# HGRN2 heads ahead of mLSTM heads in a hybrid decoder layer, and two raw tiles for the down factors

## The chip, the cores and the metric

The kernel runs on one core of a Trainium2 chip. The metric is the device time of one execution in microseconds, the median of several. Five engines work side by side, each through its own instructions in program order: TensorE (PE; its weight loads are PEld), VectorE (DVE), ScalarE (ACT), GpSimd (POOL) and SyncE (SP), which issues most DMAs.

## The reference

One step of a decoder layer: 1024 prompt positions and 8 decode sequences of 4 positions, 1056 columns in all. Width 1024, feed-forward width 2816, all in fp32. The mixer has four mLSTM heads and four HGRN2 heads side by side, 128 wide each:

```python
h = _rmsnorm(x, norm_mix)
p = jnp.einsum('btd,dp->btp', h, w_in) + b_in
qk_a, v_a, o_a, i_a, f_a, q_b, f_b, i_b, g_b = jnp.split(p, offs, axis=-1)
out_a, buf, C, n, m = _mlstm_mixer(qk_a, v_a, o_a, i_a, f_a, conv_buf, C0, n0, m0, conv_w, conv_b, mlstm_norm)
out_b, S = _hgrn_mixer(q_b, f_b, i_b, g_b, S0, lb, hgrn_norm)
mix = jnp.concatenate([out_a, out_b], axis=-1).astype(x.dtype)
x = x + jnp.einsum('btm,md->btd', mix, w_out)
h2 = _rmsnorm(x, norm_ffn)
ff = jax.nn.silu(jnp.einsum('btd,df->btf', h2, w_gate)) * jnp.einsum('btd,df->btf', h2, w_up)
x = x + jnp.einsum('btf,fd->btd', ff, w_down)
```

An mLSTM head passes q and k through a causal convolution of width 4 and a silu, and scans a matrix memory with input and forget gates that all four heads share (`i_raw`, `f_raw`, with a log-sigmoid and a running maximum). An HGRN2 head scans a state whose decay is its own for each feature (`f = lb + (1 - lb) * sigmoid`). Both end in a head norm and an output gate. The outputs are the final norm of x and all states, for the prompt and for the decode sequences.

## The kernel before

**Columns and units.** The 1056 columns stand in three blocks of 288 (256 prompt and the 32 decode columns), 384 and 384. An fp32 product is made of three matmuls of rounded halves (L135 hi by hi, L136 lo by hi, L137 hi by lo). A *unit* is one tile of 128 output features by one block: 8 slices of the contraction by 3, 24 matmuls. When a unit is done its `evac` moves it out of PSUM and its `post` may start a generator.

**Order.** The program is written out once by Python, and that order is the order on every engine. Side work (norms, gates, mixers, preparation of factors) is a set of generators. `hook()` is called every two slices, four times a unit; a generator that said `yield n` goes on n hooks later. `finish(key)` runs hooks until a generator is done. So a row's place on DVE or ACT follows from its number of hooks behind a unit, and what stands ahead of it there is done ahead of it.

**Stages.** Startup norms the three blocks of x: block 0 at once (`startup0`), 1 and 2 by `startup(1)` and `startup(2)` beside the first units. 99 units follow: the gate tile and 16 tiles of the mLSTM heads, then 16 tiles of the HGRN2 heads, each for three blocks. Of a head and block, the units are q, k, v, o (mLSTM) or f, q, v, g (HGRN2). Then come w_out (from the constant `first_wo`), two plain feed-forward pairs and 20 feature tiles in a two-level Winograd scheme (gate and up from about 700 us, then down), and a final norm.

**Around the change.** `gates(ps, b)` (L288) turns the gate unit of a block into log-decays (L308 to L310 on ACT: Abs, Exp, Ln; L312 to L329 on DVE, with scans), exponentials (L331 to L333) and columns by PE transposes (L343 to L346). Its numbers of hooks are `GAW`. `conv` (L432) makes q and k: three DVE rows (L445), a tanh (L449) and L450. `mix_a(h, b)` scans a block of an mLSTM head, 20 hooks long in its last row of `MAW`; its state update is L557 and L559, its products with the state L570 and L572. `mix_b(h, b)` does so for an HGRN2 head in 32 hooks: pairwise steps at levels 1, 2, 4 up to 64, each of two DVE rows (L794 on q, L796 on k, with a small row L802), and PE products for each level (L775, L853, L858), transposes of k (L875), the state's input (L889) and the products with it (L909, L911). `sample_a` and `sample_b` do the decode columns through `sample_core`, with state loads, products (L644, L672) and updates (L649) for each of 8 sequences. In before `sample_a` makes its updates at once and `sample_b` puts them off to the w_out units.

In the Winograd stage `wd_prep` prepares the factors of w_down: 20 groups, each with one load of 512 KB to the tile `fr` (L1389), four roundings on ACT to tiles `fh` (L1396), their rests on DVE (L1401) and stores to DRAM (L1402), and additions on DVE between them. `fr` has one buffer, so the load of a group is issued when the last one's reads are done, `WDY[2]` = 5 hooks ahead of its first rounding. `fh` has three.

Of the kernel before, what the change touches and what calls it, by code (L numbers as in the profile page):

```python
# [40 lines left out]
def hybrid_step(ctx: ExitStack, tc: tile.TileContext, i, o):  # L41
# [244 lines left out]
    GAW = ((1, 6, 14), (2, 3, 6), (2, 3, 6))  # L286

    def gates(ps, b):  # L288
# [15 lines left out]
        while b == 0 and ("cv", "k") not in done:  # L304
            yield 1
# [31 lines left out]
        if b == 0:  # L337
            start(gates_sample(ig, lf), ("gsm",), 40)
# [14 lines left out]
    def gates_sample(ig, lf):  # L353
# [36 lines left out]
        for a in ATs + ADs:  # L390
            nc.gpsimd.memset(a, 0.0)
# [10 lines left out]
    ss_ = {n_: mp.tile([128, 4, 32], F32, name=n_) for n_ in ("sq", "sk", "sv", "so")}  # L402

    def conv_evac(kind, h, b):
        j = h if kind == "q" else 4 + h

        def ev(ps):
            n, npr = BL[b], NPR[b]
            raw = mp.tile([128, 387], F32, tag="raw", name="raw", bufs=2)
            if kind == "q" and b and (h or b == 2):  # L410
                finish(("pS", h, b - 1))
            acc = early(kind, h, b)
            if acc is None:
                acc = tl("c" + kind, 384, 1 if kind == "q" else 2)
# [8 lines left out]
            if (h, b) == (0, 0):  # L423
                start(conv(kind, h, b, raw, acc, rs), ("cv", kind), 1)
            else:
                for _ in conv(kind, h, b, raw, acc, rs):
                    pass
        return ev

    def conv(kind, h, b, raw, acc, rs):  # L430
        j = h if kind == "q" else 4 + h
        n, npr = BL[b], NPR[b]  # L432
        while ("rs", 2) not in done:
            yield 1
# [16 lines left out]
        if b == 0:  # L451
            nc.gpsimd.tensor_copy(ss_["s" + kind][:, h, :], acc[:, 256:288])

    def early(name, h, b):
        if (name, h, b) == ("v", 0, 0):
            return ktm.rearrange("p h t -> p (h t)")
        if name != "q" or h or b == 2:
            return None
        return mp.tile([128, 4, 130], F32, tag="st", name="st", bufs=2).rearrange("p a c -> p (a c)")

    def act_evac(name, tag, func, bj, h, b, bufs=1, silu=False):
        def ev(ps):
            n = BL[b]
            t = early(name, h, b)
            if t is None:
                t = tl(tag, 384, bufs)
# [8 lines left out]
            if b == 0 and name in ("v", "o"):  # L475
                nc.gpsimd.tensor_copy(ss_["s" + name][:, h, :], t[:, 256:288])
# [13 lines left out]
    def norm_cols(s, sqs, nch, d2=None, p=128):  # L490
# [9 lines left out]
    MAW = (  # L500
# [4 lines left out]

    def mix_a(h, b):
        w = MAW[b if h == 0 else 3]
# [3 lines left out]
        while ("gc", b) not in done or ("cv", "k") not in done:  # L511
            yield 1
# [22 lines left out]
        if (h, b) == (0, 0):  # L535
            nc.gpsimd.memset(ktm, 0.0)
# [53 lines left out]
        nc.vector.scalar_tensor_tensor(mo(b)[:, h, :], pH[:, :npr], col(V_MN + h), S["o", h, b][:, :npr],  # L590
# [75 lines left out]

# [33 lines left out]
    def sample_a():  # L700
        qS, kS = ss_["sq"], ss_["sk"]
# [17 lines left out]
        for h in range(H):  # L719
# [12 lines left out]
    atn = [0]  # L732
    gS = mp.tile([128, 4, 8], F32, name="gS")
# [13 lines left out]
    def mix_b(h, b):  # L747
# [8 lines left out]
        qB, kB = tl("qB"), tl("kB")  # L756
# [62 lines left out]
        if samp:  # L819
            while ("sa",) not in done:  # L820
                yield 1
            nc.vector.tensor_copy(ss_["sk"][:, h, :], kB[:, 256:288])
            nc.vector.tensor_copy(gS[:, h, :], gx[:, gst[1] + 64:gst[1] + 72])
            nc.vector.tensor_copy(ss_["sq"][:, h, :], qB[:, 256:288])
# [56 lines left out]
        if samp:  # L881
            nc.gpsimd.tensor_copy(ss_["sv"][:, h, :], v[:, 256:288])
            nc.gpsimd.tensor_copy(ss_["so"][:, h, :], S["g", h, b][:, 256:288])
# [44 lines left out]
        nc.vector.scalar_tensor_tensor(mo(b)[:, 4 + h, :], pH[:, :npr], col(V_HN + h), S["g", h, b][:, :npr],  # L928
                                       op0=OP.mult, op1=OP.mult)

    def sample_b():
        yield from sample_core(4, 128, V_HN, i["S0"], lambda h, s: gS[:, h, s:s + 1], o["Ss"], None, None, None,
                               later=("su",))
# [12 lines left out]
    ti = 0  # L946
    wa = i["wA"]
    tg = wtile(wa[0])
# [1009 lines left out]
```

## Time and profile before

| | |
|---|---|
| median of 3 runs | 1400.34 us (1400.12 to 1401.76) |
| profiled execution, its own time | 1404.88 us |
| span of its profile | 1403.1 us |
| mean granted TensorE clock | 0.978 |
| the first mLSTM head, all three blocks | within the first 130 us |
| first `fr` load to last | 742.1 to 1068.9 us |

Busy is the time in which an engine worked. The granted clock is TensorE's, 1.00 for full speed; at 0.50 a matmul takes twice as long and still counts as busy. A list of waits says which engine and line stood idle, what released it, how long in all, how often, and the longest. The rows that matter are shown in the prediction.

### The profile page before, as it was taken

The page shows a single profiled execution, that of the slowest core. Times are in us where ns is not written, and L with a number is a line of the kernel's source. Part 1 is how long each engine was busy: PE and PEld are TensorE (multiplying, and loading weights), DVE is VectorE, ACT ScalarE, POOL GpSimd, SP SyncE. Part 2 cuts the span into 40 slices and gives each one's busy share as a digit, 9 for nine tenths or more (in the row PEclk, how much of TensorE's full clock was granted, in tenths as well). Part 3 has the DMA queues.
Part 4 walks back from the last instruction along what each step waited for, and adds up shares of the span by engine and source line. Part 5 has one row for each costly group of instructions (what it writes and reads, how often), then busy time and mean ns, then how long its engine had stood idle before and what let it go on. Part 6 is the DMA issues. An engine that isn't in the chain of part 4 may idle for free. (4 is left out here: it accounts for less than half of the span.)

```text
span 1403.1 us, 29356 instructions
## 1 busy us (share of the span) xinstructions
PE 1338.5 (95%) x11600; PEld 1305.5 (93%) x11600; DVE 882.1 (63%) x2060; ACT 554.3 (40%) x1315; POOL 593.6 (42%) x566
## 2 busy tenths in 40 slices
PE   7888999999999999999989999999999999999996
PEld 6778999899999997999989999999999999999995
DVE  7876657664555556634576666666775346777765
ACT  6554334234334335323444544444444341122232
POOL 5223212232222314123447656665655683444434
PEclk8999999999999999999999999999999999999997
DMA  6012122330111114543544656756656278878733
GB/s 224 23 43 70 53 60 73 96 99 21 44 47 34 39 41 131 155 152 124 185 146 174 245 189 215 247 193 215 235 176 224 77 260 319 308 269 299 274 143 124
DMA packets 108882, 212.11 MB, mean 151 GB/s; under 512 B 10801, under 2 KB 63561, under 8 KB 108233
## 3 DMA queue, kind: packets, MB, share of 16 engines
q1 hardware_dynamic: 108312, 209.98, 43.6%
q8 instruction: 91, 1.49, 0.4%
q14 instruction: 47, 0.38, 0.1%
q10 hardware_dynamic: 432, 0.27, 0.1%
HBM read 143.76 MB, written 66.45 MB: 150 GB/s over the span
## 5 line engine op out<-in xcount | busy, mean ns | idle before, releaser
L135 PE MATMUL mm<-HI,whi 128*128 128x384 f32 (+2 forms) x1160 | 379.1, 327 | 6.6 <-ACT gA L302 2.9
L137 PE MATMUL mm<-HI,wlo 128*128 128x384 f32 (+2 forms) x1160 | 363.2, 313 | 1.3 <-POOL wlo L97 1.3
L136 PE MATMUL mm<-LO,whi 128*128 128x384 f32 (+2 forms) x1160 | 363.0, 313 | 0.5 <-POOL LO L225 0.2
L135 PEld LDWEIGHTS mm<-HI,whi 128*128 128x128 f32 x1160 | 221.5, 191 | 11.8 <-ACT gA L302 3.2
L136 PEld LDWEIGHTS mm<-LO,whi 128*128 128x128 f32 x1160 | 221.5, 191 | 1.4 <-POOL LO L225 0.9
L137 PEld LDWEIGHTS mm<-HI,wlo 128*128 128x128 f32 x1160 | 221.2, 191 | 1.8 <-POOL wlo L97 1.8
L97 POOL TENSOR_TENSOR wlo<-raw,whi 128x512 fp32r<-128x512 f32 x90 | 118.7, 1329 | 214.7 <-ACT whi L96 169.8
L1189 POOL TENSOR_TENSOR wlo<-S,whi 128x512 fp32r<-128x512 f32 x78 | 108.4, 1396 | 112.2 <-ACT whi L1188 102.1
L1260 PE MATMUL mx<-T,whi 128*128 128x264 f32 x640 | 118.4, 284 | 1.7 <-DVE sg L1227 0.9
L1401 DVE TENSOR_TENSOR fh<-fr,fh 128x512 fp32r<-128x512 f32 x80 | 76.4, 959 | 68.3 <-ACT fh L1396 67.6
L1260 PEld LDWEIGHTS mx<-T,whi 128*128 128x128 f32 x640 | 99.0, 188 | 2.1 <-DVE sg L1227 1.1
L1313 POOL TENSOR_TENSOR LO<-rg,HI 128x528 fp32r<-128x528 f32 x52 | 70.5, 1367 | 65.4 <-ACT HI L1312 65.4
L1260 PE MATMUL mx<-HI,whi 128*128 128x264 f32 x320 | 92.1, 288 | 4.1 <-ACT u L1268 4.1
L1260 PE MATMUL mx<-HI,wlo 128*128 128x264 f32 x320 | 91.6, 286 | 0.0
L1260 PE MATMUL mx<-LO,whi 128*128 128x264 f32 x320 | 91.4, 286 | 0.0
L1260 PE MATMUL mx<-T,wlo 128*128 128x264 f32 x320 | 90.8, 284 | 0.0
L1487 DVE TENSOR_TENSOR X<-X,mx 128x264 f32<-128x264 f32 x160 | 65.5, 425 | 27.2 <-PE mx L1483 26.7
L1188 ACT ACTIVATE whi<-S 128x512 fp32r<-128x512 f32 x80 | 50.3, 631 | 73.4 <-DVE S L1177 73.4
L1312 ACT ACTIVATE HI<-rg 128x528 fp32r<-128x528 f32 x52 | 32.3, 641 | 104.6 <-PE mx L1483 34.1
L1396 ACT ACTIVATE fh<-fr 128x512 fp32r<-128x512 f32 x80 | 45.3, 571 | 69.6 <-DMA fr<-in_wd 43.0
L1260 PE MATMUL mm<-HI,wlo 128*128 128x264 f32 x240 | 68.2, 284 | 0.0
L1260 PE MATMUL mm<-HI,whi 128*128 128x264 f32 x240 | 68.2, 284 | 0.0
(545 smaller groups left out, 3449.6 us busy)
## 6 DMA issues: line engine op xcount, KB each, us to landing
d_wf<-fh SPq DMA_DIRECT2D x60, 512.0 KB
rg<-d_ff SPq DMA_DIRECT2D x42, 528.0 KB
raw<-in_wA SPq DMA_DIRECT2D x31, 512.0 KB
whi<-d_wf SPq DMA_DIRECT2D x29, 512.0 KB
wlo<-d_wf SPq DMA_DIRECT2D x28, 512.0 KB
raw<-in_wgu SPq DMA_DIRECT2D x24, 512.0 KB
d_ff<-sg SPq DMA_DIRECT2D x40, 264.0 KB
rg<-in_wgu SPq DMA_DIRECT2D x20, 512.0 KB
```

The source lines that it names most:

```text
L97: (nc.gpsimd if pool else nc.vector).tensor_tensor(lo[:, s], raw[:, s], hi[:, s].bitcast(F32), op=OP.subtract)
L135: nc.tensor.matmul(ps[:, :n], wh, rh[:, k, :], start=(k == 0), stop=False)
L136: nc.tensor.matmul(ps[:, :n], wh, rl[:, k, :], start=False, stop=False)
L137: nc.tensor.matmul(ps[:, :n], wl, rh[:, k, :], start=False, stop=(k == nk - 1))
L1188: nc.scalar.activation(hi[:, s], t, AF.Copy)
L1189: (nc.vector if dve else nc.gpsimd).tensor_tensor(lo[:, s], t, hi[:, s].bitcast(F32), op=OP.subtract)
L1260: nc.tensor.matmul(ps[:, :QN], a[:, w], b_[:, kk, c], start=new and kk == 0 and x == 0, stop=kk == 3 and x == 2, skip_group_check=True)
L1312: nc.scalar.activation(h, src, AF.Copy)
L1313: (nc.vector if dve else nc.gpsimd).tensor_tensor(lw, src, h.bitcast(F32), op=OP.subtract)
L1396: nc.scalar.activation(h, src, AF.Copy)
L1401: nc.vector.tensor_tensor(lw, src, h.bitcast(F32), op=OP.subtract)
L1487: nc.vector.tensor_tensor(y, y, ps[:, :QN], op=OP.add)
```

## The change

The units of the HGRN2 heads come first (48 units) and the gate tile and mLSTM heads behind them. The host orders the weight tiles, w_out's rows and so the features of `X` to match. `sample_b` starts four units ahead of the first mLSTM unit, with its state updates at once; `sample_a` waits for it, and puts its updates off. `gates` has tiles of its own and one row of hooks for all blocks, `mix_a` one row for all heads, `conv` runs at once in the evacuation. The norms of blocks 1 and 2 must be done at units 4 and 8 (5 and 10), and their squares use other scratch. Apart from that, `wd_prep` has two `fr` tiles and loads a group right behind the first store of the group before; `fh` has two buffers, and a group one hook less.

```diff
@@ -283,26 +283,18 @@
-    GAW = ((1, 6, 14), (2, 3, 6), (2, 3, 6))
+    GAW = ((2, 3, 6), (2, 3, 6), (2, 3, 6))
...
         lo, hi = slice(0, 4), slice(32, 36)
-        if b == 0:
-            A, B = (a.rearrange("p c t -> p (c t)") for a in ATs)
-            Cc, me = (mp.tile([128, 3, 130], F32, tag="C", name="C", bufs=2).rearrange("p a c -> p (a c)")
-                      for _ in range(2))
-            me = me[0:4]
-        else:
-            A, B, Cc = (mp.tile([36, 384], F32, tag=x, name=x) for x in ("gA", "gB", "gC"))
-            me = mp.tile([4, 385], F32, tag="gm", name="gm")
+        A, B, Cc = (mp.tile([36, 384], F32, tag=x, name=x, bufs=nb) for x, nb in (("gA", 2), ("gB", 2), ("gC", 1)))
+        me = mp.tile([4, 385], F32, tag="gm", name="gm", bufs=1)
         ig, f, lf, a = A[lo, :n], A[hi, :n], B[lo, :n], B[hi, :n]
...
         yield 1
-        while b == 0 and ("cv", "k") not in done:
-            yield 1
         while b and ("pS", 0, b - 1) not in done:
@@ -335,7 +327,7 @@
-            start(gates_sample(ig, lf), ("gsm",), 40)
+            start(gates_sample(ig, lf), ("gsm",), 4)
...
@@ -420,18 +408,12 @@
-            if (h, b) == (0, 0):
-                start(conv(kind, h, b, raw, acc, rs), ("cv", kind), 1)
-            else:
-                for _ in conv(kind, h, b, raw, acc, rs):
-                    pass
+            conv(kind, h, b, raw, acc, rs)
...
-        while ("rs", 2) not in done:
-            yield 1
...
@@ -497,18 +470,14 @@
-    MAW = (
-        (1, 1, 3, 3, 2, 2, 2, 6, 1),
-        (2, 3, 3, 1, 2, 4, 1, 7, 3),
-        (3, 1, 3, 1, 2, 2, 2, 4, 1),
-        (2, 1, 3, 1, 2, 2, 2, 6, 1))
+    MAW = (2, 1, 3, 1, 2, 2, 2, 6, 1)
...
-        w = MAW[b if h == 0 else 3]
+        w = MAW
...
-        while ("gc", b) not in done or ("cv", "k") not in done:
+        while ("gc", b) not in done:
@@ -532,8 +501,8 @@
-        if (h, b) == (0, 0):
-            nc.gpsimd.memset(ktm, 0.0)
+        while (h, b) == (0, 0) and ("b", H - 1, 2) not in done:
+            yield 1
...
@@ -596,10 +565,11 @@
-    def sample_core(h_off, w, vnorm, st_in, decay, out_state, n_io, d2, k_scale, later=None):
-        qS, kS, vS, oS = (ss_[x] for x in ("sq", "sk", "sv", "so"))
+    nc.gpsimd.memset(ktm, 0.0)
+    def sample_core(ss, h_off, w, vnorm, st_in, decay, out_state, n_io, d2, k_scale, later=None, end=None):
+        qS, kS, vS, oS = (ss[x] for x in ("sq", "sk", "sv", "so"))
@@ -658,11 +628,15 @@
                 nc.vector.tensor_scalar_mul(vm[:, 0:w], vt[:, 0:w], seqm[:, s:s + 1])
+                if w == 129:
+                    nc.gpsimd.tensor_copy(sts[s][:, :, 128:129], n_io[0][:, 4 * s:4 * s + 4, None])
                 yield 3
...
                 yield 3
+            if end is not None:
+                end()
@@ -698,7 +672,9 @@
-        qS, kS = ss_["sq"], ss_["sk"]
+        while ("sb",) not in done:
+            yield 1
+        qS, kS = ssA["sq"], ssA["sk"]
@@ -721,15 +697,17 @@
-        yield from sample_core(0, 129, V_MN, i["C0"], lambda h, s: wiS[:, 32 * h + 4 * s + 3:32 * h + 4 * s + 4],
-                               o["Cs"], (nT, no), scol[:, 1:2], scol[:, 2:3])
-        nc.sync.dma_start(o["ns"], no)
+        yield from sample_core(ssA, 4, 129, V_MN, i["C0"], lambda h, s: wiS[:, 32 * h + 4 * s + 3:32 * h + 4 * s + 4],
+                               o["Cs"], (nT, no), scol[:, 1:2], scol[:, 2:3], later=("su",),
+                               end=lambda: nc.sync.dma_start(o["ns"], no))
...
+    for a in ATs + ADs:
+        nc.gpsimd.memset(a, 0.0)
...
@@ -943,32 +918,32 @@
-    ti = 0
...
-    tg = wtile(wa[0])
...
-        ts = [wtile(wa[1 + 4 * h + j]) for j in range(4)]
+        ts = [wtile(wa[4 * h + j]) for j in range(4)]
+        for b in range(NB):
+            evs = [f_evac(h, b), act_evac("qb", "cq", AF.Sigmoid, V_BIN + 16 + h, h, b, 2, silu=True),
+                   act_evac("vb", "v", AF.Identity, V_BIN + 24 + h, h, b, 2),
+                   act_evac("g", "go", AF.Sigmoid, V_BIN + 28 + h, h, b, 2, silu=True)]
+            posts = [None, spawn((lambda h, b: lambda: mix_b(h, b))(h, b), "b", h, b), None, None]
+            in_group(ts, b, evs, posts, (("mm", "mm", "mx", "mx") if (h, b) == (0, 0) else None))
+    first_a = len(units)
+    tg = wtile(wa[16])
+    for h in range(H):
+        ts = [wtile(wa[17 + 4 * h + j]) for j in range(4)]
...
-                   act_evac("v", "v", AF.Identity, V_BIN + 8 + h, h, b),
+                   act_evac("v", "v", AF.Identity, V_BIN + 8 + h, h, b, 2),
...
-            in_group(ts, b, evs, posts, (("mm", "mm", "mx", "mx") if (h, b) == (0, 0) else None))
+            in_group(ts, b, evs, posts)
...
-    for h in range(H):
-        ts = [wtile(wa[17 + 4 * h + j]) for j in range(4)]
-        for b in range(NB):
-            evs = [f_evac(h, b), act_evac("qb", "cq", AF.Sigmoid, V_BIN + 16 + h, h, b, silu=True),
-                   act_evac("vb", "v", AF.Identity, V_BIN + 24 + h, h, b),
-                   act_evac("g", "go", AF.Sigmoid, V_BIN + 28 + h, h, b, 2, silu=True)]
-            posts = [None, spawn((lambda h, b: lambda: mix_b(h, b))(h, b), "b", h, b), None, None]
-            in_group(ts, b, evs, posts)
...
@@ -1384,14 +1359,14 @@
         def fload(g):
-            t = fpool[0].tile([128, 4, 256], F32, tag="fr", name="fr", bufs=1)
+            t = fpool[0].tile([128, 4, 256], F32, tag="fr", name="fr", bufs=2)
             f = NPLAIN + 4 * (g // 4)
...
             n = 128 * src.shape[1]
-            t = fpool[0].tile([128, 1024], F32R, tag="fh", name="fh", bufs=3)
+            t = fpool[0].tile([128, 1024], F32R, tag="fh", name="fh", bufs=2)
             h, lw = (x.rearrange("p (f c) -> p f c", c=128) for x in (t[:, 0:n], t[:, n:2 * n]))
@@ -1400,14 +1375,17 @@
             nc.sync.dma_start(d_wf[g, k, :, 0:2 * n], t[:, 0:2 * n].bitcast(F32))
-        r = fload(0)
+        nxt = fload(0)
         yield WDY[0]
         for g in range(NG):
+            r = nxt
             left, right = r[:, :, 0:128], r[:, :, 128:256]
...
             rest(g, 0, left, p)
+            if g + 1 < NG:
+                nxt = fload(g + 1)
             p = rnd(a22)
@@ -1425,12 +1403,9 @@
-            yield WDY[1]
-            if g + 1 < NG:
-                r = fload(g + 1)
...
-    WDY = (2, 2, 5)
+    WDY = (2, 2, 6)
@@ -1667,12 +1642,12 @@
-        acc = (ntile("W") if b == 1 else tl("vt", 390, 1))[:, :n]
+        acc = ntile()[:, :n]
...
-            sq = tl(*SQT[(0, 1, 6, 7)[m % 4]])[:, :n]
+            sq = (ntile("raw") if m % 4 < 2 else tl("qB"))[:, :n]
...
@@ -1826,13 +1800,11 @@
             finish(("w", u["t"]))
-        if ui in (5, 10):
-            finish(("n1", ui // 5))
-        if ui == b0_first - 8:
-            lb_consts()
-        if ui == b0_first + 4:
-            finish(("sa",))
-        if ui == b0_first + 12 * (H - 1) + 8:
+        if ui in (4, 8):
+            finish(("n1", ui // 4))
+        if ui == first_a - 8:
+            conv_consts()
+        if ui == first_a - 4:
             start(sample_b(), ("sb",))
...
```

DVE in the first 60 us. Before, behind norm 1 (L228, L225), the convolution of the first head's q follows:

```order
L225 TENSOR_TENSOR LO<-X,HI 128x384
L228 SCALAR_TENSOR_TENSOR X<-X,vec,mx 128x384 x2
L225 TENSOR_TENSOR LO<-X,HI 128x384
L209 TENSOR_SCALAR nrs<-mx 128x3
L435 COPY raw<-hist 128x3
```

The same place of the change (`nt` is the sum of squares of block 2, `qw`, `ck`, `qB`, `kB` are q and k of `mix_b`):

```order
L209 TENSOR_SCALAR nrs<-mx 128x3
L1653 TENSOR_TENSOR nt<-raw 128x384
L1653 TENSOR_TENSOR nt<-nt,qB 128x384 x2
L1653 TENSOR_TENSOR nt<-nt,raw 128x384 x2
L1653 TENSOR_TENSOR nt<-nt,qB 128x384 x2
L789 COPY_PREDICATED AD_127<-msk,mx 128x64
...
L772 TENSOR_TENSOR qw<-qw,ngb 128x144
L774 TENSOR_TENSOR ck<-ck,ngb 128x144
L780 TENSOR_TENSOR wib<-ngb 128x144
...
L228 SCALAR_TENSOR_TENSOR X<-X,vec,mx 128x384 x2
```

Seven sum rows stand ahead of the first steps of `mix_b(0, 0)` (L772, L774), and these ahead of norm 1 (L228).

DVE of the change at units 49 and 50, where the first gates (`gA`, `gB`, `gC`, `gm`) meet the end of the last `mix_b` (in before the first gates met a convolution there):

```order
L619 SCALAR_TENSOR_TENSOR st<-st,gS,mx 128x128 x4
L304 SCALAR_TENSOR_TENSOR gB<-gA,gB 4x288
L305 COPY gm<-mcar 4x1
L309 SCALAR_TENSOR_TENSOR gC<-ones,gB 4x128 x2
L311 SCALAR_TENSOR_TENSOR gm<-gB,mcar,gA 4x256
L312 COPY mcar<-gm 4x1
...
L321 TENSOR_TENSOR gA<-gA,gC 4x256
L772 TENSOR_TENSOR qB<-qB,wib 128x3x64
L774 TENSOR_TENSOR kB<-kB,wib 128x3x64
L780 TENSOR_TENSOR wib<-wib 128x3
L417 COPY raw<-hist 128x3
```

The step at level 64 (L772, L774) stands behind the gates and behind an update of `sample_b` (L619), and the convolution of q (from L417) behind it. On PE the transposes of that kB (L851) come at U50.

SP in the Winograd stage, before:

```order
L1389 DMA fr<-in_wd 128x4x256
L1402 DMA d_wf<-fh 128x1024
L1402 DMA d_wf<-fh 128x512
L1241 DMA d_ff<-sg 128x528
L1402 DMA d_wf<-fh 128x1024 x2
L1389 DMA fr<-in_wd 128x4x256
```

and now:

```order
L1364 DMA fr<-in_wd 128x4x256
L1377 DMA d_wf<-fh 128x1024
L1364 DMA fr<-in_wd 128x4x256
L1377 DMA d_wf<-fh 128x512
L1216 DMA d_ff<-sg 128x528
L1377 DMA d_wf<-fh 128x1024 x2
```

The load of the next group moves from behind a group's four stores to behind its first.

More of the change, by code (lines that the diff above doesn't have):

```diff
@@ L409, in ev @@
             raw = mp.tile([128, 387], F32, tag="raw", name="raw", bufs=2)
[L410 to L414, printed above, removed]
+            if kind == "q" and b == 2:
+                finish(("pS", h, 0))
+            acc = tl("c" + kind, 384, 2)
             S[kind, h, b] = acc
@@ L819, in mix_b @@
         if samp:
-            while ("sa",) not in done:
-                yield 1
-            nc.vector.tensor_copy(ss_["sk"][:, h, :], kB[:, 256:288])
+            nc.vector.tensor_copy(ssB["sk"][:, h, :], kB[:, 256:288])
             nc.vector.tensor_copy(gS[:, h, :], gx[:, gst[1] + 64:gst[1] + 72])
-            nc.vector.tensor_copy(ss_["sq"][:, h, :], qB[:, 256:288])
+            nc.vector.tensor_copy(ssB["sq"][:, h, :], qB[:, 256:288])
         yield 2
@@ L988, in mix_split @@
         for m in range(KT):
-            while any(("a" if m < 4 else "b", m % 4, b) not in done for b in range(2 + th)):
+            while any(("b" if m < 4 else "a", m % 4, b) not in done for b in range(2 + th)):
                 yield 2
@@ L998, in mix_split @@
         if th:
-            while ("sb",) not in done:
+            while ("sa",) not in done:
                 yield 1
@@ L1712, in hybrid_step @@
     startup0()
-    conv_consts()
+    lb_consts()
     for _ in split(1, True):
@@ L1912, in _prepare @@
     idx = [4 * g + h for h in range(4) for g in range(4)] + [16 + 4 * g + h for h in range(4) for g in (1, 0, 2, 3)]
-    wA = np.concatenate([tiles(gate), wt[idx]], axis=0)
+    wA = np.concatenate([wt[idx[16:]], tiles(gate), wt[idx[:16]]], axis=0)
     bg = np.zeros((128, 1), b_in.dtype)
```

34 lines of the change are left out of this document (11 added, 23 removed).

## The prediction

> **What bounds the kernel now.** I read the page's first part, then busy time by stretches of 50 us, then TensorE's waits in the stretches that are not full. Columns of the stretches: length, then busy time and number of instructions of PE, PEld, DVE, ACT and POOL, granted clock, DMA share, GB/s.
>
> ```profile
> PE 1338.5 (95%) x11600; PEld 1305.5 (93%) x11600; DVE 882.1 (63%) x2060; ACT 554.3 (40%) x1315; POOL 593.6 (42%) x566
> 50.00:100.00 50.00, 38.15 (x217) 36.08 (x216) 37.91 (x83) 30.97 (x58) 12.38 (x16) 0.90 0.06 14
> 100.00:150.00 50.00, 44.94 (x298) 43.91 (x297) 33.10 (x103) 20.49 (x58) 13.41 (x21) 0.97 0.27 82
> 150.00:200.00 50.00, 50.00 (x338) 49.94 (x337) 32.84 (x88) 19.70 (x55) 13.66 (x18) 1.00 0.20 60
> 250.00:300.00 50.00, 47.33 (x354) 43.65 (x353) 33.31 (x100) 15.80 (x38) 17.37 (x41) 1.00 0.41 125
> 300.00:350.00 50.00, 48.45 (x567) 45.91 (x566) 25.01 (x99) 18.31 (x60) 9.70 (x12) 1.00 0.08 24
> 400.00:450.00 50.00, 49.74 (x631) 47.41 (x632) 27.69 (x104) 21.98 (x69) 14.21 (x13) 1.00 0.11 35
> 550.00:600.00 50.00, 48.05 (x489) 45.76 (x490) 30.76 (x97) 18.15 (x53) 9.40 (x13) 0.97 0.51 152
> ```
>
> TensorE bounds it: 95% busy, and full at 150 to 200. The change has no other matmuls, so it can only move the places where PE idles or runs at a lower clock. The largest is the first mLSTM head: 50 to 100 lacks 11.9 us and 100 to 150 lacks 5.1. The clock costs 38.15 x 0.10 = 3.8 and 44.94 x 0.03 = 1.3. That is **22.1 us** in all, 5.1 of clock on 17.0 of idleness: 0.30 us of clock for each idle us. The HGRN2 heads (400 to 450) lack 0.3 in 50. DVE works 33 us in 50 in an mLSTM stretch and 26 to 28 in an HGRN2 one. The waits in the poor place (waited in all, times, longest):
>
> ```profile
> PE mx L572 <- DVE C L557: 3.7, 1, 3.7
> PE mm L135 <- ACT gA L302: 2.9, 1, 2.9
> PE mx L549 <- issue: 1.8, 1, 1.8
> PE mx L344 <- ACT gB L332: 3.4, 1, 3.4
> ```
>
> L135 and L344 wait for the gates; L572 for an mLSTM state behind DVE's convolution. They belong to the first mLSTM head while DVE is also making norms.
>
> **The change, part by part.** I write U50 for the point at which 50 units are done. Each sum is made against the profiled execution (1404.88 us) and then added to the median (1400.34).
>
> *A, the start.* HGRN2 units now run while blocks 1 and 2 are normed. What goes is the loss behind 72.5 us, where before has done nine units:
>
> ```profile
> 75.00:80.00 5.00, 1.17 (x9) 0.97 (x8) 3.56 (x9) 2.97 (x4) 0.00 (x0) 0.98 0.00 0
> 80.00:85.00 5.00, 3.31 (x19) 3.06 (x20) 2.78 (x11) 2.37 (x8) 0.75 (x2) 0.50 0.30 77
> 85.00:90.00 5.00, 5.00 (x28) 5.00 (x27) 3.73 (x11) 1.82 (x4) 0.00 (x0) 0.84 0.03 9
> 90.00:95.00 5.00, 4.26 (x28) 4.02 (x27) 3.30 (x8) 4.87 (x9) 0.00 (x0) 1.00 0.00 0
> 105.00:110.00 5.00, 1.28 (x12) 0.93 (x11) 2.56 (x15) 3.97 (x8) 0.00 (x0) 1.00 0.05 16
> 110.00:115.00 5.00, 4.84 (x25) 4.68 (x24) 2.61 (x10) 2.59 (x13) 4.42 (x8) 0.66 0.51 157
> 115.00:120.00 5.00, 4.34 (x33) 4.11 (x33) 3.89 (x8) 2.92 (x7) 2.48 (x3) 1.00 0.08 15
> 120.00:125.00 5.00, 4.47 (x34) 4.31 (x35) 4.25 (x16) 1.47 (x4) 0.21 (x1) 1.00 0.50 157
> ```
>
> Idle: 3.8 + 1.7 + 0.7 + 3.7 + 0.2 + 0.7 + 0.5 = 11.3. Clock: 3.31 x 0.50 + 5.00 x 0.16 + 4.84 x 0.34 = 4.1. Together 15.4. An HGRN2 head with norms done should lose about 1.5 in the same work (0.3 in 50, and a little for DVE). What comes: the seven DVE rows that sum the squares of block 2 now stand ahead of the first steps of mix_b, and those steps ahead of norm 1.
>
> ```profile
> 33.04 3.03 DVE L1678 TENSOR_TENSOR vt<-vt,go 128x384 f32<-128x384 f32 x2
> ...
> 42.21 0.56 DVE L225 TENSOR_TENSOR LO<-X,HI 128x384 fp32r<-128x384 f32 x1
> L794 DVE TENSOR_TENSOR qB<-qB,wib 128x192 f32<-128x192 f32 (+1 forms) x18 | 7.4, 414 | 5.9 <-PE mx L858 5.9
> L796 DVE TENSOR_TENSOR kB<-kB,wib 128x192 f32<-128x192 f32 (+1 forms) x18 | 5.9, 328 | 0.0
> ```
>
> A sum row costs up to 1.5 us (3.03 for two), norm 1 is what stands from there to 42.77, 6.7 us, a step of mix_b some 0.9 (L794, L796 and a small row). Carrying PE and DVE through the new order with these, PE stalls about 2.5 us on the third set of steps (U3.5), 5 on the next behind norm 1 (U4.5) and 3.3 at U8. It does nine units at about 78, 5.5 later than before. The DVE rows alone, without gaps, would allow 70, 2 earlier. I take the hand count: A = 5.5 + 1.5 - 15.4 = **-8.4**; the other end is -16.
>
> *B, the changeover from HGRN2 to mLSTM (U44 to U64).* The first mLSTM head meets no norms now, but the end of the last HGRN2 head, and sample_b with its eight state updates. Before shows no such place. The rows that set it are the gates (their first and last DVE row for block 0; the wait for their logarithm in block 1, first on ACT, then on DVE) and the convolution:
>
> ```profile
> 52.03 0.45 DVE L312 SCALAR_TENSOR_TENSOR AT<-AT,AT 4x288 f32<-4x288 f32 x1 [2.24 <-ACT AT L310]
> 55.37 0.41 DVE L329 TENSOR_TENSOR AT<-AT,C 4x256 f32<-4x256 f32 x1
> 92.33 0.52 ACT L309 ACTIVATE gB<-gB 4x384 f32<-4x384 f32 x1
> 92.87 1.28 ACT L310 ACT_TABLE_LOAD   x1
> 94.72 0.55 DVE L312 SCALAR_TENSOR_TENSOR gB<-gA,gB 4x384 f32<-4x384 f32 x1
> L445 DVE SCALAR_TENSOR_TENSOR ck<-raw,vec,ck 128x384 f32<-128x384 f32 (+1 forms) x36 | 22.6, 627 | 2.2 <-ACT ck L417 1.5
> ```
>
> In the new order the gates' DVE rows for block 0 (3.8 us, 52.03 to 55.78) stand ahead of the last-but-one steps of the last mix_b. They come 3 hooks behind the gates' evacuation, some 2.4 us, in which ACT has to do two Identities, Abs, Exp and Ln with two table loads, about 4.5 us. So DVE waits for ACT, and PE's L851 (U50) for DVE's kB: 5.2 us. Behind it the same way: L865 at U50.75 waits for kt behind conv q with its tanh (3.3), L887 at U51.5 for C behind conv k (2.7), L668 at U54.25 for sjunk behind conv q of block 1 (3.5), L336 at U57.75 and U62.75 for the gates' exponentials of blocks 1 and 2 (3.5 and 3). A convolution of 384 columns holds DVE for three rows of 0.63 and more. Sum 21.2 us idle, and with 0.30 of clock for each, 27.6. The same head cost 22.1 in before; I take the middle, 24.9. From it goes before's own changeover, the 2.7 and 1.5 that 250 to 350 lack, though single waits are smaller there: B = **+20.7**. The top is 27.6 - 4.2 = +23.4, and a worse order isn't excluded. A floor comes from DVE alone: its 220 rows from U44 to U64, each as long as its like in before, make 91 us (0.41 a row; 32.84 / 88 = 0.37 at 150 to 200); twenty units take some 83 (12 in 50). The 8 us between them make 10.4 with clock, less 4.2: +6.2.
>
> The clock's part is the weakest number here. The Trainium skill ("TensorE: Matmul & The Clock Gate", Part 1: The HAM clock gate) says that the clock goes to half only after an idle window of about 3.4 us; by it, six waits set apart by a unit or more would mostly cost their own length, and B would be nearer to 17 (21.2 - 4.2). The rows agree at 80 to 85 (0.50 behind 5.5 us of idleness) and at 110 to 115 (0.66 behind 3.7). For the table loads the Trainium skill ("ScalarE: Activation LUTs", What ACT_TABLE_LOAD costs) gives 1.28 us plus a drain of 1.38, which would make U50's wait 2.8 longer. The trace leaves no room for a drain: L309 ends at 92.85, the load at 94.15, one 0.52 us activation follows, and DVE goes on at 94.72.
>
> *C, the end of the mixers.* mix_a needs 20 hooks where mix_b needs 32, so the last mixer is done before w_out's units start:
>
> ```profile
> PE mx L858 <- DVE wib L802: 3.4, 2, 1.9
> ```
>
> 1.9 of these and the 48.05 x 0.03 = 1.4 of clock in 550 to 600 go, while the other 1.5 comes back at U45 in the same kind of place. C = **-3** (0 to -4).
>
> *D, the down factors.* The wait for raw tiles on ACT, the units of PE that felt ACT late, the loads and the factors:
>
> ```profile
> ACT fh L1396 <- DMA fr<-in_wd: 43.0, 13, 6.0
> ACT fh L1396 <- issue: 19.1, 7, 4.2
> PE mx L1260 <- ACT u L1268: 4.1, 3, 2.8
> PE mx L1260 <- DVE sg L1227: 0.9, 1, 0.9
> PE mx L1260 <- DVE u L1233: 0.7, 1, 0.7
> L1389 SPq DMA_DIRECT2D fr<-in_wd x20: 384/428/1420, 742.1 to 1068.9; - x20
> L1396 ACT ACTIVATE fh<-fr 128x512 fp32r<-128x512 f32 x80 | 45.3, 571 | 69.6 <-DMA fr<-in_wd 43.0 <-issue 19.1 <-DMA d_ff<-sg 5.4
> L1401 DVE TENSOR_TENSOR fh<-fr,fh 128x512 fp32r<-128x512 f32 x80 | 76.4, 959 | 68.3 <-ACT fh L1396 67.6
> ```
>
> A group takes (1068.9 - 742.1) / 19 = 17.2 us, 23 hooks of 0.75. The load was issued 5 hooks (3.7 us) ahead, and ACT then waited 43.0 / 13 = 3.3: it lands after 7.0. Now it has 20 hooks, 15 us: all 62.1 us of ACT's waits go. PE's share of them is at most 5.7 us (4.1 + 0.9 + 0.7). One hook less a group spaces nothing else. Against it: with two fh tiles, a rounding waits for the store two factors back, 8 hooks (6.0 us) instead of 11 (8.3). Rounding and rest take 0.57 + 0.96 = 1.5; a store as slow as that load is free after 8.5, and ACT waits 2.5 us. That is 150 us over 60 big stores, and at PE's 5.7 of 62.1, 13.8. A store of 4.5 us costs nothing. I take the gain less 2.2 of such waits: D = **-3.5**, between -5.7 and +8.1.
>
> Sum: -8.4 + 20.7 - 3 - 3.5 = **+5.8**: 1410.7 for a profiled execution, 1406.1 for the median.
>
> **The rivals.**
>
> *The changeover hides its waits (faster).* My chain counts every row late that stands behind a late one. If hooks give DVE its time back, as at 400 to 450, where mix_b's steps cost 0.3 in 50, only DVE's floor stays, B = 6.2. Sum -8.4 + 6.2 - 3 - 3.5 = -8.7: **1391.6**. For it: the steady mLSTM stretch, 150 to 200, is full with 33 us of DVE. Against it: gates and convolutions of three blocks come within 16 units, as at 50 to 126.
>
> *The clock stays up (no change).* The waits stand as I count them, but each is too short to lower the clock: B = 21.2 - 4.2 = 17.0, sum +2.1: **1402.4**. For it: 90 to 95 and 115 to 125 lost 0.5 to 0.7 us each with 1.00 granted. Against it: 110 to 115, above. This is what the rule of the Trainium skill on the clock gate, named above, would give.
>
> *Two fh tiles turn the load's wait into the store's (slower).* It decides from a store that takes over 4.5 us (6.0 - 1.5). With the 7.0 of the loads, D = +8.1, sum +17.4: **1417.7**. For it: DVE's 68.3 us of idleness shows rounding and store on a tight chain. Against it: ACT is 40% busy and PE reads its factors much later.
>
> **How the numbers follow.** Forecast 1406.1 with 0.38, faster rival 0.33, no change 0.17, store waits 0.12. A measurement of this kernel tells about 0.2%, 2.8 us, from no change. So slower is 0.38 + 0.12 = 0.50, same 0.17, faster 0.33. A at its other end (-16) takes 7.6 from any of these, to 1384 in the faster case; store waits with B at its top give 1420. I leave out a tenth at each side: 1387 to 1420. The forecast's own range is 1403.1, where slower begins, to 1408.8 (B at 23.4).
>
> **What would show it.** A: the first 80 us with PE waits at L753 for DVE rows 772 and 774, and no wait of over 1 us from 85 to 190 us. B: between 200 and 300 us waits of 3 to 5 us at L851, L865, L887, L668 and L336, some 21 in all, and a clock under 1.00 in those stretches; fewer than 10 would make the faster rival true. C: no wait at L829 within 20 us of w_out's first unit. D: no ACT wait for fr; waits of ACT for d_wf's stores only if the last rival is true. My forecast is wrong if the changeover costs under 12 us, or the start is not 8 us better.

## The result, and the profile after

The changed kernel takes 1422.45 us (median of 4 runs, 1421.79 to 1425.03), where before takes 1400.23 in the runs beside it: a ratio of **1.0163** (95% interval 1.0145 to 1.018), 22 us slower. The forecast was 1406.1 in a range of 1387 to 1420. The sign was right, the size four times too small, and the range was just missed.

The line of the engines and the stretches after, with the columns of the prediction, and behind them the first stretch of before, which the prediction did not show:

```profile
PE 1348.0 (95%) x11600; PEld 1315.8 (93%) x11600; DVE 865.9 (61%) x2060; ACT 560.1 (39%) x1316; POOL 593.3 (42%) x574
0.00:50.00 50.00, 36.32 (x268) 32.72 (x269) 38.73 (x97) 28.61 (x59) 23.75 (x30) 0.89 0.45 158
50.00:100.00 50.00, 45.42 (x505) 43.12 (x505) 29.79 (x78) 21.40 (x61) 20.35 (x20) 0.90 0.10 33
300.00:350.00 50.00, 39.11 (x290) 35.92 (x289) 26.98 (x107) 18.85 (x48) 4.68 (x14) 0.90 0.23 61
350.00:400.00 50.00, 38.93 (x232) 37.99 (x231) 27.65 (x64) 23.79 (x49) 7.13 (x7) 0.91 0.10 30
400.00:450.00 50.00, 49.39 (x317) 48.51 (x317) 27.06 (x82) 17.95 (x47) 9.99 (x15) 0.92 0.19 63
550.00:600.00 50.00, 42.96 (x295) 40.19 (x294) 31.58 (x80) 20.71 (x48) 15.15 (x27) 0.90 0.45 133
1000.00:1050.00 50.00, 50.00 (x414) 50.00 (x413) 32.16 (x56) 23.93 (x52) 31.12 (x25) 1.00 0.61 214
```

```profile
0.00:50.00 50.00, 40.75 (x232) 37.61 (x233) 38.82 (x84) 29.52 (x61) 24.83 (x29) 0.86 0.48 168
```

I add what PE lacks and what it lost by the clock (busy time by one less the granted clock). In the first 150 us before lost 9.3 + 5.7 and the 22.1 of the prediction, 37 us. After loses 13.7 + 4.0 and 4.6 + 4.5 in the first 100 and 0.1 in the next 50: 27. So the start is 10 better. From 300 to 450 after loses 10.9 + 3.9, 11.1 + 3.5 and 0.6 + 4.0: 34, where before lost 2. At 550 to 600 it loses 7.0 + 4.3. At 1000 to 1050 PE is full, where before lacked 0.9.

TensorE's waits after, from 300 to 420, then from 560 to 620 us (waited in all, times, longest):

```profile
PE mx L557 <- DVE kt L552: 8.1, 1, 8.1
PE mx L851 <- DVE kB L774: 4.9, 1, 4.9
PE mx L668 <- DVE sjunk L665: 3.7, 1, 3.7
PE mx L336 <- ACT gB L324: 2.6, 1, 2.6
PE mx L336 <- DVE st L619: 1.0, 1, 1.0
PE mx L887 <- DVE C L875: 0.7, 1, 0.7
```

```profile
PE mx L668 <- DVE sjunk L665: 6.7, 1, 6.7
```

L851, the first L668 and the first L336 are where the prediction put them, with about its lengths (5.2, 3.5, 3.5). Two more of its waits are all but missing: L865 (3.3) does not wait, and L887 (2.7) waits 0.7. The largest, L557, is not in its list, nor is the second L668. What held L557 up is seen on DVE from 385 us on (start, length, row, idle before):

```profile
385.43 0.64 DVE L548 TENSOR_TENSOR sm<-sm,cols 128x3 f32<-128x3 f32 x1 [5.03 <-ACT sm L545]
...
387.63 0.55 DVE L304 SCALAR_TENSOR_TENSOR gB<-gA,gB 4x384 f32<-4x384 f32 x1
...
394.16 0.55 DVE L321 TENSOR_TENSOR gA<-gA,gC 4x384 f32<-4x384 f32 x1
...
395.01 1.93 DVE L427 SCALAR_TENSOR_TENSOR ck<-raw,vec,ck 128x384 f32<-128x384 f32 x3
398.86 0.56 DVE L432 SCALAR_TENSOR_TENSOR ck<-raw,ck 128x384 f32<-128x384 f32 x1 [1.93 <-ACT raw L431]
399.33 0.86 DVE L552 TENSOR_SCALAR kt<-mx,sm 128x128 f32<-128x128 f32 x3
```

The head norm of block 1 (L552) stands behind the gates of block 2 (7.1 us, L304 to L321) and behind a convolution with a table load (4.7 us), and PE behind it.

### The profile page after: what moved, and what is told of

Same layout as the page of the kernel before. It is cut to its first block, busy times and chain, and to the rows that moved or that the text cites. A ratio compares the mean times of both kernels' runs of the same rounds, so it can differ in the third digit from the quotient of the medians.

```text
span 1420.5 us, 29401 instructions
## 1 busy us (share of the span) xinstructions
PE 1348.0 (95%) x11600; PEld 1315.8 (93%) x11600; DVE 865.9 (61%) x2060; ACT 560.1 (39%) x1316; POOL 593.3 (42%) x574
## 4 chain that ended last, share of the span: by engine, by line
PE 78%; DVE 11%; ACT 5%; issue 3%; DMA 2%; POOL 1%; SPq 0%; POOLq 0%; DVEq 0%; ACTq 0%
PE mx L1235 16%; PE mm L135 10%; PE mm L1235 9%; PE mm L137 9%; PE mm L136 9%; PE mx L1458 8%; PE mm L1458 5%; PE so L1235 3%; PE mx L753 1%; PE so L1458 1%; DMA rg<-d_ff 1%; PE mx L614 1%; ACT HI L229 1%; DVE X L228 1%; DVE nt L1653 1%
## 5 line engine op out<-in xcount | busy, mean ns | idle before, releaser
L1376 DVE TENSOR_TENSOR fh<-fr,fh 128x512 fp32r<-128x512 f32 x80 | 67.0, 838 | 33.8 <-ACT fh L1371 33.6
L1235 PE MATMUL mm<-LO,whi 128*128 128x264 f32 x240 | 67.9, 283 | 0.0
```

Of the source, the lines that this page charges most:

```text
L1235: nc.tensor.matmul(ps[:, :QN], a[:, w], b_[:, kk, c], start=new and kk == 0 and x == 0, stop=kk == 3 and x == 2, skip_group_check=True)
L1376: nc.vector.tensor_tensor(lw, src, h.bitcast(F32), op=OP.subtract)
```

## Experiments

Ratios are to before, run beside each kernel. How much a run gains on the change is the difference of the two ratios by 1400 us; by the intervals each such gain is good to about 4 us either way, so a gain of 4 to 6 us alone does not decide between a theory and a rival that lie this close.

**The down factors alone**: before with the new `wd_prep`.

```diff
-            t = fpool[0].tile([128, 4, 256], F32, tag="fr", name="fr", bufs=1)
+            t = fpool[0].tile([128, 4, 256], F32, tag="fr", name="fr", bufs=2)
...
-            t = fpool[0].tile([128, 1024], F32R, tag="fh", name="fh", bufs=3)
+            t = fpool[0].tile([128, 1024], F32R, tag="fh", name="fh", bufs=2)
```

> The order of before, with the change's preparation of the down factors alone (two raw tiles, load a group ahead, two fh tiles). Theory 'the load's wait goes': in the profile of the change ACT waits no more for raw tiles and PE's waits of 5.7 us on L1260's side are gone, with 1.4 us of clock at 1050 to 1100. Expected 6 us faster than before, about 1394 (0.4%). Rival 'store waits': 2 to 8 us slower, 1402 to 1408, with ACT waits on the stores.

1393.63 us, ratio **0.9937** (0.9923 to 0.9951), 8 us faster by the medians. It is faster than both kernels. ACT's rows on `fh`:

```profile
ACT fh L1396 <- DMA d_wf<-fh: 21.2, 13, 4.4
```

The rival's waits for stores are there, 1.6 us each on average. They cost PE nothing: from 740 to 1100 us it has no wait at all in this run.

**The order alone**: the change with the old `wd_prep`.

> The change with the preparation of the down factors of before: order of heads alone. Theory 'all of the loss is in the changeover': 6 us over the change, about 1428. Rival 'the factors cost time': under 1420.

1430.19 us, ratio 1.0204 (1.0181 to 1.0227). In this order the new `wd_prep` is worth 1.0204 - 1.0163, 6 us. The two parts add up within the noise: 1.0204 - 0.0063 = 1.0141, and 1.0163 was measured with an interval that all but reaches it. All of the loss is the order's.

**A gap behind the decode norm's row.**

```diff
         nc.vector.tensor_scalar_mul(hn, pO[:, 0:128], sm[:, 2, 0:1])
-        yield 1
+        yield 5
```

> The change, with 5 hooks in place of 1 between the decode norm's last DVE row (L665) and its transposes on PE (L668), in sample_a and sample_b. Theory 'PE stands behind a row that stands behind a convolution': both waits (3.7 and 6.7 us) go, and with them some 2.4 us of clock at 345 and 4.3 at 580 to 600, 12 to 17 us in all: 1405 to 1410. Rival 'DVE is late as a whole': PE waits for the next DVE rows instead, at most 4 us faster.

1419.64 us, ratio 1.0122 (1.0102 to 1.0142): 6 us, where 12 to 17 were expected and the rival had 4. In place of L668 PE waits for the next rows that stand behind the same convolutions (320 to 420, then 560 to 620):

```profile
PE mx L518 <- DVE kt L510: 2.5, 1, 2.5
```

```profile
PE mx L614 <- DVE svm L630: 6.0, 2, 5.7
```

**The first head's hooks of before.**

```diff
-    MAW = (2, 1, 3, 1, 2, 2, 2, 6, 1)
+    MAW = (
+        (1, 1, 3, 3, 2, 2, 2, 6, 1),
+        (2, 3, 3, 1, 2, 4, 1, 7, 3),
+        (3, 1, 3, 1, 2, 2, 2, 4, 1),
+        (2, 1, 3, 1, 2, 2, 2, 6, 1))
...
-        w = MAW
+        w = MAW[b if h == 0 else 3]
```

> The change, with the four rows of hooks of before for the first mLSTM head. Theory 'order': L557's transposes of block 1 stand 4 hooks (some 4 us) later behind the same DVE rows, its wait of 8.1 us falls to about 4, with 2 us less clock: 4 to 7 us faster, 1415 to 1418. Rival 'DVE is late as a whole': PE waits as long elsewhere in the same head, within 2 us of the change.

1420.11 us, ratio 1.0124 (1.0106 to 1.0143): 5 us, the theory's number, but by a mixture of theory and rival. The 8.1 us are gone altogether, and 5.7 of them come back: the gates' own reader now waits twice (6.5 for 2.6), and another row 1.8 (320 to 420; lines are 4 higher there behind the table):

```profile
PE mx L336 <- ACT gB L324: 6.5, 2, 4.4
PE mx L522 <- DVE kt L514: 1.8, 1, 1.8
```

**Without sample_b's updates.**

```diff
             if later is None:
-                yield from update(s, vms[s])
+                yield 1
+                nc.sync.dma_start(out_state[s].rearrange("h k v -> k h v"), st[:, :, 0:128])
```

> The change, with the eight state updates of sample_b left out (32 products on PE and 32 rows on DVE, 11 us of DVE; the states are stored as they were loaded). Theory 'order': the rows that PE waits for stand behind gates and convolutions, not behind the updates; L851, L557 and L336 keep their waits, 1 to 5 us faster than the change, 1418 to 1421. Rival 'DVE has too much to do there': the waits shrink by the 11 us, with clock 14 or more: under 1409.

1415.82 us, ratio 1.0105 (1.0081 to 1.0129): 8 us, between the two theories. The waits at L557 (8.1), L668 (3.7 and 6.7) and L336 (2.6) stand unchanged, and L851's (L852 there) is 5.5; so the updates do not feed these waits. The gain goes with the 11 us of DVE rows and the products on PE that are left out, not with these waits; where it comes from was not followed further.

**The gates 12 units earlier**, beside the last HGRN2 head.

```diff
+        if h == H - 1:
+            tg = wtile(wa[16])
         ts = [wtile(wa[4 * h + j]) for j in range(4)]
...
+            if h == H - 1:
+                unit(tg, hrhs(b), KT, gates_evac(b))
+                units.insert(gu, units.pop())
```

> The change, with the gate tile's three units 12 units earlier, beside the last HGRN2 head, and the broadcast of the first head's gates loaded with its q. Theory 'order': DVE idles 20 us in 50 there, so the gates' rows and table loads cost nothing; L336's 3.9 us and L557's 8.1 go, L851's 4.9 falls to 2 or 3 (the convolution of q then stands ahead of its row); with clock 18 to 24 us faster than the change, 1398 to 1404. Rival: the gates' rows delay mix_b's steps as much, waits at L753 and L829 of the last HGRN2 head: over 1414.

1416.19 us, ratio 1.0109 (1.0088 to 1.013): 8 us of 18 to 24. L557 and L336 are gone, and the rival comes true: the gates now hold up the last HGRN2 head. L851's wait has only moved with them (lines are 3 lower in this run: L848 is L851, L862 is L865, L884 is L887). DVE stands still for the logarithm of the first gates, and the step at level 64 behind their rows:

```profile
236.65 0.45 DVE L302 SCALAR_TENSOR_TENSOR gB<-gA,gB 4x288 f32<-4x288 f32 x1 [6.03 <-ACT gB L300]
...
240.71 0.35 DVE L771 TENSOR_TENSOR kB<-kB,wib 128x192 f32<-128x192 f32 x1
```

ACT's table loads in this run, by line:

```profile
L442 ACT ACT_TABLE_LOAD x6 | 7.7, 1283 | 0.1
L299 ACT ACT_TABLE_LOAD x3 | 3.8, 1283 | 0.1
L300 ACT ACT_TABLE_LOAD x3 | 3.8, 1283 | 0.1
L321 ACT ACT_TABLE_LOAD x3 | 3.8, 1283 | 0.1
L716 ACT ACT_TABLE_LOAD x2 | 2.6, 1283 | 0.0
```

These 17 are of 22 in the program; the change has 11. Each of the gates' exponentials and logarithms now stands between sigmoids, and PE waits there, from 200 to 300 and 300 to 420:

```profile
PE mx L848 <- DVE wib L777: 5.5, 1, 5.5
PE mx L862 <- ACT vt L852: 2.3, 1, 2.3
```

```profile
PE mx L884 <- DVE C L872: 3.1, 1, 3.1
```

**The norm row one hook earlier.**

```diff
-        yield 2
+        yield 1
         nc.vector.tensor_scalar_mul(hn, pO[:, 0:128], sm[:, 2, 0:1])
-        yield 1
+        yield 2
```

> The change, with the decode norm's last DVE row (L665) one hook earlier, ahead of the convolution, and its reader on PE (L668) where it was. Theory 'order': the wait of 3.7 us at L668 goes for good, with 2 of clock; that of 6.7 in the last mLSTM units turns into one of some 5.7 at the next row behind the same convolution (the first update's L614): 4 to 7 us faster than the change. Rival 'DVE is late as a whole': under 3.

1419.3 us, ratio 1.0124 (1.0099 to 1.0149): 5 us, the theory's number, though not by its steps. In the last mLSTM units 6.7 us fell to 1.9 and 2.3 at two readers; at the first place L668 is held for 3.0 us by another chain behind the same convolution (ACT's vt, L509, that comes behind its tanh).

**Gates early, norm row early and the first update later.**

> The change with the gates as in the run before last, the norm row as in the run before, and the first update of sample_a 4 hooks later, so that its products no longer stand right behind a convolution. If the three causes add up, the waits of 5.7 to 6.7 us in the last mLSTM units go as well, with 4 of clock: 28 to 36 us faster than the change, 1386 to 1394, which is as fast as the order of before with the new down factors (1393.6) or faster. If they do not add up, 1398 to 1404.

1416.26 us, ratio 1.0108 (1.0088 to 1.0129): nothing beyond the early gates alone. They did not add up.

**The first gates' rows 3 hooks later** (`GAW[0]` = (5, 3, 6)).

> The change, with the first gates' DVE rows 3 hooks later, behind the last step of mix_b (L772, level 64) and the convolution of q. Theory 'order': L851's wait of 4.9 us goes, with 1 us of clock (310 to 320): 5 to 6 us faster than the change, 1416 to 1418. Rival 'the gates' chain blocks whatever comes next': L865 or L887 wait instead, under 2 us faster.

1419.24 us, ratio 1.0132 (1.0116 to 1.0148): 4 us, between theory and rival. L851 no longer waits; L614, one hook behind it, does:

```profile
PE mx L614 <- ACT vt L855: 4.4, 1, 4.4
```

**Without the gates' work.** The constants come from POOL.

```diff
-        nc.scalar.activation(a, f, AF.Abs)
-        nc.scalar.activation(a, a, AF.Exp, scale=-1.0)
-        nc.scalar.activation(a, a, AF.Ln, bias=1.0)
...
+        for x in (ng, lf, wl, m):
+            nc.gpsimd.memset(x, -1.0)
```

> The change, with the gates' logarithm (three ACT rows and their table loads) and their DVE rows left out in all three blocks; POOL fills the tiles with constants. Theory 'the gates' chain is what the changeover costs': L851's 4.9, L336's 3.9 and L557's 8.1 us go, with 6.6 us of clock behind them (310 to 320, 365 to 370, 390 to 410): 20 to 24 us faster than the change, 1398 to 1402. Rival 'convolutions and the last HGRN2 head are as much in the way': 10 us faster or less.

1401.06 us, ratio 0.9998 (0.9989 to 1.0008): 0.0165 under the change, 23 us, as the theory has it. PE's longest waits from 250 to 420 us are now the decode norm (L668, 17 lines lower here) and an update:

```profile
PE mx L651 <- DVE sjunk L648: 3.7, 1, 3.7
PE mx L597 <- ACT vt L838: 1.6, 1, 1.6
```

The gates are what holds L851, L336 (but for 1.0 us) and L557 up.

**Without the logarithm's table loads** (an Identity in place of Ln).

> The change, with an Identity in place of the gates' logarithm: the loads of its table (3) and of the table behind it (3) go, nothing else. Theory 'each load stands in a chain that PE waits for': 1.3 us less at L851, at one L336 and at L557, and with two loads (its own and the one at tanh) up to 2.6 each; 4 to 8 us faster than the change with clock, 1414 to 1418. Rival 'the loads lie beside other work': within 2 us.

1413.08 us, ratio 1.008 (1.0053 to 1.0107): 12 us, more than the 4 to 8 expected. The waits at L557 (8.1 to 5.5), L851 (4.9 to 3.6) and L336 (2.6 to none) shrink by one load of 1.28 us or by two.

**Four edits of hooks together.**

> The change with four edits of hooks together: the first gates' rows later, the first head's mix_a with the rows of before, the norm row one hook earlier, the first update of sample_a 4 hooks later. If the gains add up: 5 + 2 + 3 + 3, 1408 to 1411. If a wait that goes only comes back at the next reader: 1414 to 1418. Neither reaches the order of before with the new down factors (1393.6).

1413.61 us, ratio 1.0097 (1.0076 to 1.0118): 9 us of the 13 that they would add up to.

**Before without the gates' work**, the same edit.

> The order of before, with the gates' logarithm and DVE rows left out as in the run of the change. It tells what the same work costs in its old place. By the waits there (2.9 at L135 for gA, 3.4 and 0.3 at L344 and L345, with 1.7 to 2.5 us of clock behind them) 7 to 10 us faster than before, 1390 to 1394; then the new place costs 11 to 14 us more (21.4 in all). Rival 'the gates cost as much in either place': 18 us or more, under 1383; then the loss of the changeover has another cause.

1382.57 us, ratio **0.9854** (0.9831 to 0.9876): 20 us, and the rival holds: the gates cost as much in either place (20 and 23 us are not told apart). So moving them makes at most a few us of the order's loss; the new place pays for them what the old one did. The start of before without gates:

```profile
0.00:50.00 50.00, 41.21 (x222) 38.83 (x223) 37.49 (x84) 29.26 (x60) 24.66 (x28) 0.93 0.48 168
50.00:100.00 50.00, 47.18 (x311) 45.69 (x309) 35.92 (x88) 26.07 (x65) 23.01 (x36) 1.00 0.19 54
100.00:150.00 50.00, 48.80 (x323) 48.34 (x322) 31.85 (x90) 19.85 (x56) 10.25 (x16) 1.00 0.18 54
```

It loses 8.8 + 2.9 + 2.8 + 1.2, 16 us, where before lost 37. From 50 to 150 us it is 4 where before lost 22: the first mLSTM head beside the norms runs nearly free, and what made this stretch of before poor was the gates.

**The gates' DVE rows in two pieces** on top of the four edits (a `yield 1` behind the scans).

> The change with the four edits of hooks together as before, and the gates' DVE rows cut in two pieces a hook apart, so that steps and head norms come between them. If the length of the piece counts: 2 to 5 us faster than the four edits alone, 1408 to 1411. If ACT's chain of loads counts: within 2 us of them, 1412 to 1416.

1414.15 us, ratio 1.0082 (1.0058 to 1.0106), not told apart from the four edits alone.

**Without the gates' work, norm row early, first update later.**

> The change without the gates' work, with the norm row a hook earlier and the first update of sample_a 4 hooks later. What is left beside gates and decode norms is the start and the down factors: by the stretches of the two profiles 10 and 8 us better than before. Expected 7 to 10 us under the change without the gates' work (3.7 and 6.7 of waits, part of which comes back): 1391 to 1394. Rival 'DVE is late as a whole': 1397 or more.

1396.12 us, ratio 0.9946 (0.9927 to 0.9965): 7 us under the change without gates by the ratios, as the theory has it; the time itself lies between the theory's 1394 and the rival's 1397. The norm row alone was worth 5 us beside the gates, and with the later update nothing on top of the early gates.

**The sums of block 2's squares 8 hooks later** (`yield 18` for `yield 10`).

> The change, with the sums of squares of block 2 starting 8 hooks later, behind the first steps of mix_b(0, 0) and behind norm 1. Theory 'the seven sum rows ahead of the steps hold the start up': the waits at L753 (1.5, 2.5 and 0.7 us in the first 50 us) shrink by 3 to 5 us, with clock 4 to 6 us faster than the change, 1416 to 1418. Rival 'DVE is full in the first 70 us, whatever the order': the rows come back ahead of norm 2, within 2 us of the change.

1428.77 us, ratio 1.0189 (1.0172 to 1.0207): 4 us slower than the change, barely clear of the noise and outside both theories. The steps now stand behind the norms' own rows: L753 waits 2.8 us behind norm 1 (at 47 us) and L829 3.4 behind norm 2 (at 78). Later is no better for the sums.

**The new down factors, the gates' differences on POOL** (L325 to L329 in the order of before).

> The order of before with the new down factors, and the gates' four differences (L325 to L329) on POOL in place of DVE. The gates cost 20 us there, of which these rows are 1.6 us on DVE for block 0 and 3 for each of the others. Theory 'what holds DVE counts': 2 to 5 us faster than the new down factors alone, 1389 to 1392 (ratio 0.990 to 0.992). Rival 'the chain's length counts': POOL is slower a row, same or up to 3 us slower (0.994 to 0.996).

1393.62 us, ratio 0.9941 (0.9925 to 0.9957), the same as the new down factors alone, as the rival has it.

## Why the forecast was half right

**A, the start**: -8.4 was said, 10 was found (37 to 27). The size was right by luck: the reason was wrong. The prediction laid the loss of before to "the first mLSTM head while DVE is also making norms", though two waits of its own list (2.9 and 3.4) were for the gates. Without gates the first 150 us lose 16, 21 less; 18 of these lie in its poor place from 50 to 150, so there it was the gates and not the norms. The other 3 lie in the first 50 us, nearly all in the clock, and the clock there varies as much by itself: the change and 13 runs with the same start lose 26 to 32 us in 150, most of the spread in the first 50, at a clock of 0.75 to 0.91. The HGRN2 head in the place of the mLSTM head loses 27, 11 more than an mLSTM head without gates. So, good to a few us each, the change takes 21 us of gates out of the start and puts 11 us of steps behind norms in. The hand count of these steps had that about right (5.5 us late, and the loss of the first 72 us kept).

**B, the changeover**: 20.7 was said, and 300 to 450 loses 34 where before lost 2, and 250 to 300 is 1.3 better: 30.5. This is the step that failed, by 10 us. Its idle sum held: 21.2 said, 22.6 found. What did not:
- The clock. 0.30 us of clock for each idle us was taken from 50 to 150 of before; here 11.4 us go with 22.6, 0.50 each.
- "I take the middle of the two": the chain's 27.6 was averaged down to 24.9 with the 22.1 of before, as if the old place were a milder instance. It was not: the gates cost 0.0146 of the time in before (20 us) and 0.0165 in the change (23), and the changeover has other waits on top.
- The chain itself missed 1.4 us of idleness.

That the idle sum held is in part luck. L851, L668 and the first L336 were found with about their lengths, but the 6.0 us of L865 and L887 came to 0.7, and the third gates' 3 us at L336 became 8.1 at L557, since the head norm of the block before stands behind the same rows: the two misses cancel.

**C, the end of the mixers**: -3 was said, and 450 to 700 loses 12.3 where before lost 7.9 (2.5, 2.0 + 1.4, 1.6 and 0.3): +4.5, a miss of 7 us and the second step that failed. L668 behind a convolution was counted for sample_b and not for sample_a, which now ends among mLSTM units too, where in before it ended the same way among HGRN2 units without convolutions (PE waited 0.6 us there, at L694). 6.7 us and 4.3 of clock are that wait.

**D, the down factors**: -3.5 was said, -8 measured (0.9937; 6 us in the changed order), within the mechanism and beyond the lower end of -5.7. The load's waits went with all PE waits of that stage, and 1.4 us of clock at 1050 to 1100, which the sum forgot. The 2.2 us kept back for stores were not needed.

Put together: -10 + 30.5 + 4.5 - 8 = +17, about the 17.4 by which the spans differ (1420.5 and 1403.1). The medians differ by 22. The prediction made its sum against one profiled execution of before, at 1404.88 us, and added it to the median, 4.5 us lower; of the change the profiled execution (1422.39) is at the median. So of the 16 us between 1406.1 and 1422.45 nearly 12 are missed in the terms. The rest is that one execution, which ran longer than the median; why it did is not shown.

**The rivals.** That the changeover hides its waits is refuted by L851, L336 and L557. That the clock stays up is refuted by 0.90 to 0.92 from 300 to 450; three of the six waits that it counted (5.2, 3.5 and 3.5) were about as long as the 3.7 us that it had against it, or longer. The stores' waits exist (20 us of ACT) and cost PE nothing.

**What stays open.** Without gates the change is still 0.0144 slower than before without them, 20 us, or 28 with the 8 that the down factors give back. By the profiles 11 of these lie at the start, 7 are decode norms (the run with the norm row early, the first update later and no gates shows these), and the rest is put down to single waits between 300 and 450 us. So the cause of this larger part of the loss is read from the profiles and, but for the 7, not shown by a run. Why HGRN2 steps beside the norms lose 11 more was not isolated: moving the sums later did not help. No order of hooks that was tried brought the changed order below before; the best of them that leaves nothing out stands at 1.0082. The version to keep is the old order with the new down factors.

## What to carry to other kernels

Before moving a stage, leave out the small serial piece next to it, once in the old place and once in the new: here the gates, four rows of logits with a chain of table loads and scans, cost 20 to 23 us in either place, and they, not the head beside them, made the poor stretch of the start of before. On engines that work in order, a wait removed by a hook came back in most tries, whole or in part, at the next reader behind the same rows; look for the row that holds the queue, not for the one that waits. Here a prefetch paid because its wait had reached the bounding engine, even though a new wait took its place on another.

## What the runs showed of the hardware

The clock falls behind single waits, one pair of them only 3 us long together. Stretches of 5 us of the change:

```profile
310.00:315.00 5.00, 2.83 (x17) 2.18 (x17) 4.14 (x17) 0.56 (x1) 0.00 (x0) 0.72 0.18 53
315.00:320.00 5.00, 4.40 (x35) 4.21 (x32) 2.76 (x9) 2.68 (x6) 0.65 (x3) 0.94 0.16 47
340.00:345.00 5.00, 1.29 (x6) 1.00 (x6) 3.89 (x10) 1.26 (x3) 0.00 (x0) 0.79 0.00 0
345.00:350.00 5.00, 5.00 (x19) 5.00 (x18) 1.36 (x7) 0.00 (x0) 0.00 (x0) 0.52 0.01 3
360.00:365.00 5.00, 2.83 (x17) 2.50 (x15) 2.84 (x8) 2.88 (x9) 0.00 (x0) 1.00 0.00 0
365.00:370.00 5.00, 4.21 (x21) 4.00 (x22) 2.26 (x9) 2.23 (x5) 0.76 (x2) 0.68 0.39 80
400.00:405.00 5.00, 5.00 (x23) 4.47 (x23) 2.57 (x6) 2.47 (x5) 3.74 (x3) 0.50 0.32 108
405.00:410.00 5.00, 5.00 (x31) 5.00 (x31) 3.16 (x7) 2.00 (x4) 1.32 (x2) 0.72 0.38 138
```

Behind 3.7 us of idleness 5 us ran at 0.52, behind some 3 us (2.6 and 0.3) 4.2 us at 0.68, and behind 8.1 us, 10 us at 0.50 and 0.72: 2.4, 1.3 and 3.9 us lost. The loss does not follow the length of the wait: behind the 4.9 us of L851 (310 to 320) only 1.1 were lost. So the 0.30 us of the prediction, and the 0.50 found, for each idle us are averages over a handful of waits, and no rule. The Trainium skill ("TensorE: Matmul & The Clock Gate", Part 1: The HAM clock gate) gives an idle window of about 3.4 us for the fall to half; the waits of 3.7 and 8.1 agree, the pair of 2.6 and 0.3 fell short of it and lowered the clock all the same.
